# Projection tiles computed one token half after the other, with weight rings of 4, 4 and 2 tiles

## The chip, the cores and the metric

The kernel runs on one core of a Trainium2 chip. The metric is the time of one execution on the device in microseconds. The engines that matter are TensorE (matmuls; PE in the profile, its weight loads PEld), VectorE (DVE), ScalarE (ACT), GpSimd (POOL), and SyncE (SP), which issues all loads and stores. Each engine works through its own stream of instructions in order and waits for the others by semaphores.

## What is computed

A trunk of two layers over 1024 tokens with 1024 channels, and one RMSNorm at the end. Each layer normalises x, applies a shift and scale that depend on the conditioning vector c, makes one wide projection, feeds its columns to three causal mixers (pooling, retention, RWKV-7), gates and merges their results, projects once more and adds the result to x:

```python
h = rms_norm(x, norm_g) * (1.0 + scale) + shift
proj = h @ w_in
pool_u, pool_g, q, k, v, ret_g, rw, rw_g, gate_logits = jnp.split(proj, points, axis=-1)
o_pool = causal_pool_mixer(pool_u, pool_w, pool_scale) * jax.nn.silu(pool_g)
o_ret = retention(q, k, v, positions, ret_norm_g) * jax.nn.silu(ret_g)
o_rwkv = rwkv7_time_mix(rw, shift_mu, w0, w2, a0, a2, k_k, k_a, r_k, ln_w, ln_b) * jax.nn.silu(rw_g)
branches = jnp.stack([o_pool, o_ret, o_rwkv], axis=2)
y = jnp.einsum('btnw,nwd->btnd', branches, w_branch)
merged = jnp.sum(gates * y, axis=2)
return x + gate * (merged @ w_out)
```

The retention mixer applies a rotary embedding to q and k; the RWKV mixer carries a state along the tokens and solves a small triangular system for each chunk of 64 tokens.

## The kernel before

**Layout.** Activations lie with channels on the partitions and tokens along the free dimension, in two halves of 512 tokens (h = 0 and 1). A projection tile is 128 output channels for all 1024 tokens. For numerical accuracy each operand is kept as a high and a low part (`hi`, `lo`), and each product takes three matmuls (`mm1`, line 413): high by high, high weight by low activation, low weight by high activation. With 8 groups of 128 input channels a tile half takes 24 matmuls of 512 columns, a tile 48.

**Weights.** A tile's weights come in two parts of 128 x 512 (j = 0 and 1, four input groups each). `wprep` (line 377) prepares the next tile: for each part a load into a raw tile (tag `wr`, line 406), then `split` (line 426): a cast on ScalarE into the high part (tag `wh`) and a subtraction on POOL into the low part (tag `wl`). Each tag is a ring of three buffers, `bufs=3`. `wprep` is called once as each tile begins, so the weights of one tile are prepared while the tile before is multiplied. Other users of the rings are the loads of the small matrices for RWKV (`lora_load`, line 905), the raw weights of the startup (`wdma`, line 1023), and six tiles of conditioning weights in the startup, which borrow the rings `wh` and `wl` (line 1174). In the second layer's output projection, and for the first three tiles, the split parts go to other buffers (`wout`, `wG`, `wbig`), but the raw tile always comes from `wr`.

**Accumulators.** Results collect in PSUM in a rotation of three tiles (`acc_ps`, line 423). A tile's two halves need one each. An accumulator is free once the tile's evacuation, `evac` (line 984), has read it: for gates a tanh on ScalarE and a store; for the silu gates a tanh and a VectorE operation; for k, r, v a scaled and shifted copy; for retention's q and k (`rotary`, line 885) four VectorE operations per half (lines 891 to 894) and an addition on POOL, with sines and cosines loaded from device memory.

**Background chains.** The mixers are Python generators (`pool_task`, `ret_task`, `rwkv_task`, `rwkv_post`, `norm_task`) in lanes. After each matmul of a projection tile, `pump` (line 292) emits further steps of those whose due time has come, by a clock that counts the matmuls emitted (`mmul`, line 315) and delays that each step gives by hand. So their matmuls stand among those of the projection tiles in TensorE's stream, and their VectorE, ScalarE and POOL work among the evacuations. In the RWKV chain, after the preparation of a head (ending in products of BK and AR, lines 686 to 700, and transposes `bt`), VectorE solves the triangular systems in 30 steps (lines 756 to 766, tiles MT and tm), transposes the result (line 769), and TensorE takes it up (`m`, lines 778 to 797). In startup the order on TensorE, VectorE, ScalarE and POOL is that of the program (line 1124); after it, and for SP throughout, the framework that builds the kernel places each engine's instructions itself, by the order of the program, the buffers that are free and its own estimate of when an instruction can start.

**Stages.** The startup lasts to about 100 us. Then, for each layer, come the projection tiles with the chains in the background (lines 1274 to 1287), the merge stage (1350 to 1388), in which gate and `wg` tiles alternate with branch tiles of 48 matmuls, and the output projection (1399 to 1443), whose tiles take one token half, 24 matmuls. Projection tiles are computed by `in_tile2` (line 1267), which multiplies both halves by the weights' first part, then both by the second, and returns two accumulators; `in_tile` (line 1261) does one half and serves the first three tiles of the second layer.

Of the kernel before, what the change touches and what calls it, by code (L numbers as in the profile page):

```python
# [9 lines left out]
F32 = mybir.dt.float32  # L10
F32R = mybir.dt.float32r
# [6 lines left out]
P = 128  # L18
# [3 lines left out]
W = 512  # L22
HF = 512
# [66 lines left out]
def trunk_kernel(ctx, tc, xT, cvec, pos, vecs, consts, w_ada, w_all, pool_w, lora_w, out):  # L90
# [3 lines left out]
    wp = ctx.enter_context(tc.tile_pool(name="wp", bufs=2))  # L94
# [12 lines left out]
    def nm(s):  # L107
        uid[0] += 1
        return f"{s}_{uid[0]}"
# [26 lines left out]
    def r8(s):  # L136
        return rp.tile([P, 2048], F32, tag="r8", name=nm(s))
# [54 lines left out]
    def ada_load(l, g, slot_, ws, n):  # L192
        for _ in range(n):
            w = slot_("wada")
            nc.sync.dma_start(out=w, in_=w_ada[l, ADA[g][2] + len(ws)])
            ws.append(w)
# [131 lines left out]
    def kept(l):  # L328
        return l + 1 == L
# [47 lines left out]
    def wprep(big=False):  # L377
        for l, it in planner:
            if it != ("merge",):
                break  # L380
            wready.append((it, None))
        else:
            return
        t = None
        if it[0] == "out" and it[1] >= 2 and kept(l):
            if it[2]:
                wready.append((it, keep_w[it[1]]))
                return
            if it[1] < 6:
                t = r8("wout")  # L390
            else:
                if it[1] == 6:
                    keep_w["G"] = gp.tile([P, 32, P], F32, tag="G", name=nm("wG")).rearrange("p a b -> p (a b)")
                t = keep_w["G"][:, 2048 * (it[1] - 6) : 2048 * (it[1] - 5)]
        elif big:
            t = r8("wbig")
        parts = []
        for j in range(2):
            if t is not None:
                o = j * D  # L400
                hi, lo = t[:, o : o + HF].bitcast(F32R), t[:, o + HF : o + D].bitcast(F32R)
            else:
                hi = wp.tile([P, HF], F32R, tag="wh", name=nm("wh"), bufs=3)
                lo = wp.tile([P, HF], F32R, tag="wl", name=nm("wl"), bufs=3)
            raw = wp.tile([P, HF], F32, tag="wr", name=nm("wr"), bufs=3)
            nc.sync.dma_start(out=raw, in_=w_all[l, ITEMS.index(it[:2] if it[0] == "out" else it), j])
            split(raw, hi, lo)
            parts.append((hi, lo))
        if it[0] == "out":
            keep_w[it[1]] = parts  # L410
        wready.append((it, parts))

    def mm1(ps, w, k, r, start, stop):
        (whi, wlo), (rh, rl) = w, r
        for j, (a, b) in enumerate(((whi, rh), (whi, rl), (wlo, rh))):
            mmul(ps, a[:, k * P : (k + 1) * P], b, start=(start and j == 0), stop=(stop and j == 2))
            pump()

    def mm3(ps, w, rhs, start, stop):
        for k in range(4):  # L420
            mm1(ps, w, k, rhs[k], start and k == 0, stop and k == 3)

    def acc_ps():
        return ps_a.tile([P, HF], F32, tag="acc", name=nm("acc"))

    def split(src, hi, lo, eng=nc.gpsimd):
        nc.scalar.copy(hi, src)  # L427
        eng.tensor_tensor(lo, src, hi.bitcast(F32), op=ALU.subtract)  # L428
# [471 lines left out]
    def enter_layer(l):  # L900
        nonlocal L_
        L_ = (l, {}, {}, [])
        L_[3].extend(lora_load(l))

    def lora_load(l):
        raw = wp.tile([P, W], F32, tag="wr", name=nm("lraw"), bufs=3)
        nc.sync.dma_start(out=raw, in_=lora_w[l])
        lw = [cp.tile([P, W], F32R, tag=f"lw{j}", name=nm("lw")) for j in range(2)]
        split(raw, *lw, nc.vector)
        return lw  # L910
# [110 lines left out]
    wraw = {}  # L1021

    def wdma(j, *tiles):
        for i in tiles:
            if j == 0:
                wbig.append(r8("wbig"))
            wraw[j, i] = wp.tile([P, HF], F32, tag="wr", name=nm("wr"), bufs=3)
            nc.sync.dma_start(out=wraw[j, i], in_=w_all[0, i, j])

    def wsp(j, *tiles):  # L1030
# [93 lines left out]
    with tc.manual_schedule(engines={ET.PE, ET.DVE, ET.Activation, ET.Pool}):  # L1124
# [8 lines left out]
        aload(0, 4)  # L1133
        nc.sync.dma_start(out=vec[0], in_=vecs[0])
        wdma(0, 0)
        wsp(0, 0)
        xdma(0, 0, 1)
        wdma(0, 1, 2)
        xdma(1, 0, 1)
        aload(1, 4)  # L1140
# [19 lines left out]
        for h in range(2):  # L1160
            for kt in (2, 3):
                steps(gs[2], 2)
                scaled(h, kt)
                sq(h, kt)
        mms(0, 2, 3)
        wdma(1, 0, 1, 2)
        xdma(0, 4, 5, 6, 7)
        nc.sync.dma_start(out=cst, in_=consts[:, 0 : CST["bone"]])
# [4 lines left out]
        mms(1, 3)  # L1173
        for tag in ("wh", "wl"):
            for _ in range(3):
                w = wp.tile([P, HF], F32, tag=tag, name=nm("wada"), bufs=3)
                ada_load(0, 3, lambda _: w, aw[3], 1)
        aload(3, 2)
        for kt in range(4, 8):
# [3 lines left out]
        for kt in range(4, 8):  # L1183
            sq(1, kt)
            scaled(1, kt)
            steps(gs[3], 2)
        wprep(True)
        aload(4, 8)
        r0 = rstd_task([ssum[0]], rbc[0])
# [24 lines left out]
        next(sb)  # L1214
        first = [wready.popleft()]
        wprep()
        first.append(wready.popleft())
        pss = {}
# [24 lines left out]
    for i in range(3):  # L1243
        first_raw(1, i)
        first_evac(1, i)
    run(sb)
    L_[3].extend(lora_load(0))
    wprep()
    evac(first[0][0], pss[0, 1], 1)
    for h in range(2):  # L1250
# [5 lines left out]
    for l in range(L):  # L1256
        if l:
            enter_layer(l)
        hs = h_cur

        def in_tile(ws, h):
            ps = acc_ps()
            for j in range(2):
                mm3(ps, ws[j], hs[h][4 * j : 4 * j + 4], j == 0, j == 1)
            return ps

        def in_tile2(ws):
            pss = [acc_ps(), acc_ps()]
            for j in range(2):
                for h in range(2):  # L1270
                    mm3(pss[h], ws[j], hs[h][4 * j : 4 * j + 4], j == 0, j == 1)
            return pss

        if l:
            first = [wready.popleft() for _ in range(3)]
# [7 lines left out]
        while wready[0][0] != ("merge",):  # L1283
            it, ws = wready.popleft()
            wprep()
            for h, ps in enumerate(in_tile2(ws)):
                evac(it, ps, h)
# [62 lines left out]
        while wready[0][0][0] != "out":  # L1350
            it, ws = wready.popleft()
            prefetch()
            wprep()
            if it[0] == "wg":
                for h, ps in enumerate(in_tile2(ws)):
                    evac(it, ps, h)
            elif it[0] == "gate":
                n, d = it[1], it[2]
                for h, ps in enumerate(in_tile2(ws)):
                    nc.scalar.activation(gate_tile((n, d, h)), ps, AF.Tanh, scale=0.5)  # L1360
# [38 lines left out]
        for part, (h, sl) in enumerate(parts):  # L1399
# [3 lines left out]
            for i, d in enumerate(out_order(l, part)):  # L1403
                it, ws = wready.popleft()
# [145 lines left out]
```

## Time and profile before

| | us |
|---|---|
| median of three runs | 2542.19 |
| lowest and highest run | 2536.8, 2552.02 |
| the profiled execution | 2541.85 |
| its span, first to last instruction | 2540.1 |
| mean granted TensorE clock, share of full speed | 0.975 |

A row of the stage view gives the stretch in us, its length, for each engine its busy time and instructions, the granted clock, the share of time that the DMA engines were busy, and their rate. A row of waits gives the engine that stood idle and its line, behind the arrow what ended the idle time, then the sum in us, how many times, and the longest. A row in order of time gives start, duration, engine, line, operation, what it writes and reads, and in brackets the idle time before it and what ended that. A group or tile row gives durations in ns as least, median and greatest. Matmuls are pipelined: a matmul of 512 columns is shown as 0.39 us long, but the next begins before it ends, so the pace is read from one start to the next.

### The profile page before, as it was taken

How to read it: one execution, taken by the hardware profiler on the slowest of the kernel's cores; microseconds unless marked ns; L12 is line 12 of the kernel's file. 1: busy time of each engine (PE TensorE's matmuls, PEld its weight loads, DVE VectorE, ACT ScalarE, POOL GpSimd, SP SyncE). 2: the span in 40 equal slices, each digit the busy share in tenths (PEclk: the TensorE clock that was granted, in tenths of full speed). 3: DMA queues.
4: the chain of work that ended last, by engine and by line, in shares of the span. 5: the costliest groups of instructions: out<-in, count | busy, mean ns of one | idle time of the engine just before them, and what ended most of it. 6: DMA issues, size and time to landing. Idle time of an engine off the chain costs nothing. (4 is left out here: it accounts for less than half of the span.)

```text
span 2540.1 us, 35021 instructions
## 1 busy us (share of the span) xinstructions
PE 2421.4 (95%) x13318; PEld 1994.7 (79%) x13318; DVE 1406.1 (55%) x2618; ACT 846.9 (33%) x1530; POOL 846.7 (33%) x729
## 2 busy tenths in 40 slices
PE   6899998989899999999999999999999999999998
PEld 5677876877787788888887778778778778888888
DVE  7986579467646622444464944865783472122244
ACT  4652251333235222222354223322423433222243
POOL 5422323242123124553452313323322222445241
PEclk9899999999899899999999999999999999999999
DMA  6221111111014215663540211211111222553152
GB/s 236 71 69 59 56 42 60 35 54 51 30 51 139 94 63 185 210 193 121 174 134 26 66 35 39 63 39 59 46 42 55 83 84 71 165 159 120 58 154 75
DMA packets 125752, 226.56 MB, mean 89 GB/s; under 512 B 14224, under 2 KB 17552, under 8 KB 125584
## 3 DMA queue, kind: packets, MB, share of 16 engines
q1 hardware_dynamic: 125584, 224.32, 28.1%
q8 instruction: 105, 1.72, 0.3%
q14 instruction: 63, 0.52, 0.1%
HBM read 180.23 MB, written 44.04 MB: 88 GB/s over the span
## 5 line engine op out<-in xcount | busy, mean ns | idle before, releaser
L428 POOL TENSOR_TENSOR wl<-wr,wh 128x512 fp32r<-128x512 f32 x338 | 452.2, 1339 | 1196.0 <-ACT wh L427 1121.2
L319 PE MATMUL acc<-hhi,wh 128*128 128x512 f32 x1968 | 802.2, 408 | 13.2 <-DVE rot L894 11.2
L319 PE MATMUL acc<-hlo,wh 128*128 128x512 f32 x1968 | 802.5, 408 | 0.0
L319 PE MATMUL acc<-hhi,wl 128*128 128x512 f32 x1968 | 800.2, 407 | 0.0
L319 PEld LDWEIGHTS acc<-hhi,wh 128*128 128x128 f32 x1968 | 376.8, 191 | 82.4 <-issue 14.3
L427 ACT CAST wh<-wr 128x512 fp32r<-128x512 f32 x338 | 209.3, 620 | 693.8 <-PE acc L319 509.4
L319 PEld LDWEIGHTS acc<-hhi,wl 128*128 128x128 f32 x1968 | 376.7, 191 | 66.5 <-issue 1.8
L319 PEld LDWEIGHTS acc<-hlo,wh 128*128 128x128 f32 x1968 | 376.6, 191 | 66.5 <-issue 3.1
L319 PE MATMUL acc<-oG,wl 128*128 128x512 f32 x384 | 151.0, 393 | 0.0
L319 PE MATMUL acc<-oG,wh 128*128 128x512 f32 x384 | 151.0, 393 | 0.0
L319 PE MATMUL acc<-olo,wh 128*128 128x512 f32 x384 | 150.9, 393 | 0.0
L825 DVE TENSOR_TENSOR xst<-cy,MT 64x128 f32<-64x128 f32 x128 | 36.1, 282 | 170.2 <-PE cy L319 169.7
L836 DVE SCALAR_TENSOR_TENSOR S<-ch,pc,SP 64x64 f32<-64x64 f32 x256 | 72.4, 283 | 94.8 <-PE ch L319 90.2
L822 ACT ACTIVATE SP<-S,pc 128x128 f32<-128x128 f32 x128 | 51.4, 402 | 210.7 <-DVE S L836 197.4
L759 DVE TENSOR_TENSOR tm<-MT 64x30 f32<-64x30 f32 (+14 forms) x240 | 101.5, 423 | 7.1
L765 DVE TENSOR_TENSOR MT<-MT,tm 64x30 f32<-64x30 f32 (+14 forms) x240 | 96.3, 401 | 7.0
L1377 DVE SCALAR_TENSOR_TENSOR gs<-gs,acc 128x512 f32<-128x512 f32 x64 | 43.7, 684 | 91.7 <-PE acc L319 82.0
L319 PEld LDWEIGHTS ch<-xst,G 128*128 128x128 f32 x512 | 75.5, 191 | 15.9 <-DVE xst L825 6.6
L831 DVE COPY Z<-ch 64x128 f32<-64x128 f32 x128 | 36.0, 282 | 93.0 <-PE ch L319 92.1
L319 PEld LDWEIGHTS cy<-Z,G 128*128 128x128 f32 x512 | 76.4, 190 | 11.1
L319 PEld LDWEIGHTS acc<-oG,wl 128*128 128x128 f32 x384 | 72.1, 188 | 16.5
L319 PEld LDWEIGHTS acc<-oG,wh 128*128 128x128 f32 x384 | 72.1, 188 | 16.5
(298 smaller groups left out, 3888.9 us busy)
## 6 DMA issues: line engine op xcount, KB each, us to landing
wr<-in_w_all SPq DMA_DIRECT2D x364, 256.0 KB, 2.7
wada<-in_w_ada SPq DMA_DIRECT2D x70, 256.0 KB, 3.0
gd<-gsg SPq DMA_DIRECT2D x70, 256.0 KB, 2.0
gs<-gd SPq DMA_DIRECT2D x70, 256.0 KB, 2.8
ol<-od SPq DMA_DIRECT2D x64, 256.0 KB, 3.0
cs<-rope_d SPq DMA_DIRECT2D x32, 256.0 KB, 2.7
ringG<-in_w_ada SPq DMA_DIRECT2D x26, 256.0 KB, 5.4
x<-in_xT SPq DMA_DIRECT2D x16, 256.0 KB, 5.4
```

The source lines that it names most:

```text
L319: nc.tensor.matmul(out, lhsT=lhsT, rhs=rhs, start=start, stop=stop, **kw)
L427: nc.scalar.copy(hi, src)
L428: eng.tensor_tensor(lo, src, hi.bitcast(F32), op=ALU.subtract)
L759: nc.vector.tensor_tensor(pr, M3[:, i + 1 :, i : i + 1].to_broadcast([64, n, i]), M3[:, i : i + 1, 0:i].to_broadcast([64, n, i]), op=ALU.mult,
L765: nc.vector.tensor_tensor(M3[:, i + 1 :, 0:i], M3[:, i + 1 :, 0:i], pr, op=ALU.add)
L822: nc.scalar.activation(SP, S, AF.Copy, scale=pcc)
L825: nc.vector.tensor_tensor(xst[0:64, :], cy[0:64, 0:P], AV[:, c * P : (c + 1) * P], op=ALU.add)
L831: nc.vector.tensor_copy(Z[0:64, c, :], ch[0:64, 0:P])
L836: nc.vector.scalar_tensor_tensor(Sn[rw, rw], ch[rw, P + 64 * hd : P + 64 * hd + 64], pc[rw, c : c + 1], SP[rw, rw], op0=ALU.mult, op1=ALU.add,
L1377: nc.vector.scalar_tensor_tensor(s, s, 1.0, ps, op0=ALU.add, op1=ALU.mult)
```

## The change

`in_tile2` becomes a generator: it computes the first token half with all 24 matmuls, hands its accumulator out, and computes the second half once the caller comes back. Its callers (lines 1286, 1355, 1359) evacuate each half as they get it, so a half's evacuation is now emitted between the halves' matmuls. The accumulator of the second half is taken when its matmuls begin, not at the start of the tile. The rings `wh` and `wl` get four buffers each, the raw ring `wr` two instead of three. A buffer holds 512 values of 4 bytes per partition.

```diff
@@ -400,9 +400,9 @@
                 o = j * D
                 hi, lo = t[:, o : o + HF].bitcast(F32R), t[:, o + HF : o + D].bitcast(F32R)
             else:
-                hi = wp.tile([P, HF], F32R, tag="wh", name=nm("wh"), bufs=3)
-                lo = wp.tile([P, HF], F32R, tag="wl", name=nm("wl"), bufs=3)
-            raw = wp.tile([P, HF], F32, tag="wr", name=nm("wr"), bufs=3)
+                hi = wp.tile([P, HF], F32R, tag="wh", name=nm("wh"), bufs=4)
+                lo = wp.tile([P, HF], F32R, tag="wl", name=nm("wl"), bufs=4)
+            raw = wp.tile([P, HF], F32, tag="wr", name=nm("wr"), bufs=2)
@@ -903,7 +903,7 @@
     def lora_load(l):
-        raw = wp.tile([P, W], F32, tag="wr", name=nm("lraw"), bufs=3)
+        raw = wp.tile([P, W], F32, tag="wr", name=nm("lraw"), bufs=2)
@@ -1024,7 +1024,7 @@
-            wraw[j, i] = wp.tile([P, HF], F32, tag="wr", name=nm("wr"), bufs=3)
+            wraw[j, i] = wp.tile([P, HF], F32, tag="wr", name=nm("wr"), bufs=2)
@@ -1173,7 +1173,7 @@
         for tag in ("wh", "wl"):
             for _ in range(3):
-                w = wp.tile([P, HF], F32, tag=tag, name=nm("wada"), bufs=3)
+                w = wp.tile([P, HF], F32, tag=tag, name=nm("wada"), bufs=4)
@@ -1265,11 +1265,8 @@
         def in_tile2(ws):
-            pss = [acc_ps(), acc_ps()]
-            for j in range(2):
-                for h in range(2):
-                    mm3(pss[h], ws[j], hs[h][4 * j : 4 * j + 4], j == 0, j == 1)
-            return pss
+            for h in range(2):
+                yield in_tile(ws, h)
```

## The prediction

> **What bounds the kernel now.** I read the page first, then the busy time by stage, then who waits for whom on TensorE, then single stalls in order of time.
>
> ```profile
> span 2540.1 us, 35021 instructions
> PE 2421.4 (95%) x13318; PEld 1994.7 (79%) x13318; DVE 1406.1 (55%) x2618; ACT 846.9 (33%) x1530; POOL 846.7 (33%) x729
> core 0: us, PE busy (x) PEld busy (x) DVE busy (x) ACT busy (x) POOL busy (x), PEclk, DMA share, GB/s
> 0.00:100.00 100.00, 67.98 (x249) 53.01 (x250) 85.67 (x114) 44.74 (x74) 58.37 (x48) 0.83 0.53 182
> 100.00:900.00 800.00, 756.21 (x4421) 615.00 (x4420) 520.88 (x1022) 282.01 (x507) 221.50 (x202) 0.96 0.20 61
> 900.00:1345.00 445.00, 445.00 (x2098) 370.49 (x2097) 195.25 (x314) 136.93 (x245) 192.36 (x155) 1.00 0.49 153
> 1345.00:2100.00 755.00, 720.12 (x4337) 589.13 (x4336) 471.27 (x931) 255.56 (x463) 212.48 (x196) 0.99 0.17 54
> 2100.00:2541.00 441.00, 432.09 (x2223) 367.07 (x2221) 133.01 (x238) 127.71 (x242) 161.97 (x128) 0.99 0.38 115
> ```
>
> TensorE bounds it: 2421.4 of 2540.1 us. The edit changes no matmul, so it can win only the idle 118.7 us and the time at a reduced clock. By stage the idle time is 32.0 us in the startup (100 less 67.98), 43.8 and 34.9 us in the two projection stages (100 to 900 and 1345 to 2100), none in the first merge and output stage (445.00 of 445.00), and 8.9 us in the last window. The edit works where nothing is idle, too, but there it has nothing to win, so all that counts is the 78.7 us of the projection stages. Who TensorE waits for there:
>
> ```profile
> PE acc L319 <- DVE rot L894: 11.2, 5, 3.1
> PE bt L323 <- DVE BK L700: 9.9, 9, 2.8
> PE m L319 <- DVE MT L769: 9.6, 3, 4.7
> PE pps L319 <- DVE pdl L428: 9.4, 6, 4.7
> PE nps L319 <- DVE ksl L664: 6.8, 8, 1.8
> PE rot L323 <- DVE yc L570: 5.8, 3, 3.0
> PE acc L319 <- DVE silu L914: 1.8, 2, 1.3
> ```
>
> The first and the last row are the accumulators: a new tile half waits for a PSUM slot that VectorE has not emptied. The five rows between are the mixers' background chains: TensorE reaches a matmul of theirs before VectorE has made its input. No row has wh or wl as what TensorE waits for: the weights have never been late.
>
> **The order of the matmuls.** Three accumulators rotate. Now a tile takes two at once, and its first half ends at matmul 36 of 48; that slot is wanted again at matmul 13 of the next tile, 24 matmuls later. After the edit each half runs through its own 24 matmuls, and a slot is wanted again after the two halves that follow, 48 matmuls later. Two rows give the pace, and the stalls show what the short cycle costs:
>
> ```profile
> 1448.37 0.39 PE L319 MATMUL acc<-hhi,wh 128*128 128x512 f32 x1
> 1448.60 0.39 PE L319 MATMUL acc<-hlo,wh 128*128 128x512 f32 x1
> 1452.06 0.47 PE L319 MATMUL acc<-hhi,wh 128*128 128x512 f32 x1 [3.08 <-DVE rot L894]
> 1453.05 0.63 PE L319 MATMUL acc<-hhi,wh 128*128 128x512 f32 x1
> 1453.47 0.63 PE L319 MATMUL acc<-hlo,wh 128*128 128x512 f32 x1
> ```
>
> Start to start is 0.23 us, so the time that an evacuation has goes from 24 x 0.23 = 5.5 us to 11 us, while the longest wait is 3.1 us. All accumulator waits should vanish: 11.2 + 1.8 = 13.0 us. After the stall of 3.08 us the matmuls start 0.42 us apart instead of 0.23, and the window that holds it shows a granted clock of 0.90 (below). I count some 20 such slow matmuls behind the three longest of these stalls, 20 x 0.19 = 4 us at most.
>
> [...]
>
> **What is late next.** Three of the rot stalls' neighbourhoods, by busy time, with the stalls in them:
>
> ```profile
> 540.00:566.00 26.00, 19.56 (x88) 15.07 (x87) 25.45 (x37) 9.80 (x15) 14.60 (x12) 0.98 0.24 72
> 605.00:665.00 60.00, 49.63 (x264) 40.96 (x263) 55.20 (x104) 7.89 (x14) 16.39 (x13) 0.91 0.17 49
> 1425.00:1476.00 51.00, 41.14 (x214) 33.22 (x213) 48.73 (x89) 7.19 (x12) 16.77 (x13) 0.90 0.22 68
> 547.41 0.47 PE L319 MATMUL acc<-hhi,wh 128*128 128x512 f32 x1 [1.76 <-DVE rot L894]
> 618.50 0.47 PE L319 MATMUL acc<-hhi,wh 128*128 128x512 f32 x1 [2.68 <-DVE rot L894]
> 1435.09 0.47 PE L319 MATMUL acc<-hhi,wh 128*128 128x512 f32 x1 [2.58 <-DVE rot L894]
> 1472.21 0.99 PE L319 MATMUL m<-MT,G 32*32 32x32 f32 x25 [4.21 <-DVE MT L769]
> ```
>
> VectorE is busy for 25.45 + 55.20 + 48.73 = 129.4 of 137 us there, 94%. In the last window TensorE loses 2.58 and 3.08 us to accumulators and then 4.21 us to the end of the triangular solve (MT, lines 753 to 776), which VectorE has worked on all along. If TensorE comes there 5.66 us earlier, it waits some 5.7 us longer, unless VectorE has that much less to do before. So of the four stalls in saturated windows, 1.76 + 2.68 + 2.58 + 3.08 = 10.1 us, I give 94% back, 9.5 us: net of the accumulators 13.0 - 9.5 = 3.5 us. Bounds: 0 (all comes back) to 13.0 (nothing). Of the clock's 4 us I keep 1.5, since a stall that only moves takes its slow matmuls along; bounds 0 and 4.
>
> **The evacuations in halves.** A rotary half costs VectorE four operations, of these shapes:
>
> ```profile
> L893 DVE SCALAR_TENSOR_TENSOR rot<-acc,cs x32: 692/693/694, 273.0 to 1842.0; 64x512 f32<-64x512 f32 x32
> L894 DVE TENSOR_TENSOR rot<-acc,cs x32: 683/683/687, 273.7 to 1842.7; 64x512 f32<-64x512 f32 x32
> ```
>
> 4 x 0.69 = 2.75 us. Today both halves' evacuations are emitted behind the tile's last matmul, up to 5.5 us of VectorE in a row; after the edit it is 2.75 us twice, half a tile apart, with the chains' steps (which are emitted after every matmul) between them. The chains' waits in the list come to 9.9 + 9.6 + 9.4 + 6.8 + 5.8 = 41.5 us in 29 waits, 1.4 us each, less than the 2.75 us by which a burst shrinks; but only 16 tiles are rotary (two kinds, four heads, two layers), and where VectorE is saturated a smaller burst wins nothing. No row shows the new order, so I bound it: at best two thirds of the waits outside the solve, 2/3 x 31.9 = 21 us; at worst the same operations get ahead of the chains and cost 15 us (a rival below). I take a quarter of the 41.5, 10.4 us, nearer the gain because a burst can only get shorter.
>
> **The weight rings.** Per weight half tile: a load, a cast on ScalarE into wh, a subtraction on POOL into wl.
>
> ```profile
> ACT wh L427 <- PE acc L319: 509.4, 183, 10.7
> SPq L406 <- POOL wl L428: 1353.1, 304, 31.9
> L427 ACT CAST wh<-wr x338: 602/621/636, 76.5 to 2514.6; 128x512 fp32r<-128x512 f32 x169
> L428 POOL TENSOR_TENSOR wl<-wr,wh x338: 1255/1292/3169, 77.2 to 2515.3; 128x512 fp32r<-128x512 f32 x169
> wr<-in_w_all SPq DMA_DIRECT2D x364, 256.0 KB, 2.7
> ```
>
> With halves in sequence, the first weight half is in use up to matmul 36 instead of 24. In rings of three its successor could be cast only 12 matmuls, 2.7 us, before it is needed, against 0.62 + 1.29 = 1.9 us of work: too close. In rings of four both casts find slots that the tile before last has left, so a cast has about a tile (11 us). ScalarE then stands less often before a cast that TensorE still blocks (509.4 us in 183 waits now), which frees the silu and square operations queued behind it; I count nothing for it, since no TensorE wait above names ScalarE.
>
> The ring of raw tiles goes from three to two. A slot turns in 2.7 + 0.62 + 1.29 = 4.6 us, with the issue about 5: two slots give a raw tile every 2.5 us. Projection tiles eat one in 5.5 us. The tight place is the output stage of the first layer, 24 matmuls a tile, a raw tile every 2.72 us:
>
> ```profile
> 1228.00:1272.00 44.00, 44.00 (x203) 36.70 (x203) 12.60 (x16) 13.78 (x23) 21.66 (x17) 1.00 0.48 148
> 1234.86 3.04 SPq L406 DMA_DIRECT2D wr<-in_w_all  x2
> ```
>
> It fits by 0.2 us a tile, and the longer wh ring lets each be made 2.7 us earlier. SP runs in order, and a load that waits for its slot holds the state and gate stores behind it; it waits that way today (1353.1 us in 304 waits) without TensorE noticing. I take 0; bounds 0 and +14 us (below).
>
> In the startup the third raw load, issued at 4.97 us with the second, must now wait until POOL has split the first:
>
> ```profile
> 4.97 0.90 SPq L1028 DMA_DIRECT2D wr<-in_w_all  x2
> 8.80 1.26 POOL L428 TENSOR_TENSOR wbig<-wr,wbig 128x512 fp32r<-128x512 f32 x1 [7.59 <-ACT wbig L427]
> 17.82 0.50 PE L319 MATMUL acc<-hlo,wbig 128*128 128x512 f32 x1 [2.03 <-DVE hlo L1042]
> x<-in_xT SPq DMA_DIRECT2D x16, 256.0 KB, 5.4
> ```
>
> It goes out at 10.1 us, lands by 15.5 (5.4 us at that time of the run), and is split by 17.4, while TensorE waits for VectorE until 17.82 anyway. Behind the load on SP stand x and ada loads: if the framework leaves them there, they come up to 4.7 us late. I take +1, bounds 0 and +5.
>
> **The sum**, against the profiled execution (span 2540.1, 2541.85 us in all, 0.3 below the median 2542.19 of the runs): -3.5 - 1.5 - 10.4 + 0 + 1 = -14.4, that is 2527.5; I write **2527**. Own range 2512 to 2538.
>
> **Rivals.**
> 1. *All comes back.* VectorE sets the projection stages' pace, and the stalls only change their names. For it: 94% in the windows above. Against it: VectorE is at 520.88 of 800 us over the whole stage. The clock's 1.5 us against the startup's 1: 2541.
> 2. *The chains lose their place* (slower). First-half evacuations are now emitted ahead of all chain steps that fall into the second half, and VectorE runs in order: a solve step or BK product that fed a matmul in the second half waits up to 2.75 us more at a rotary tile. 16 tiles x 2.75 = 44 us at most; a third of it, 14.7, gives 2556. It decides once the chain has less than 2.75 us in hand, and the waits above say that it often has none. Against it: the second half's burst shrinks by as much.
> 3. *Two raw slots are too few* (slower). If a slot's turn exceeds 2 x 2.72 = 5.44 us, at 6.0 (a late landing, SP held by a store, a POOL subtraction at its 3.17 us) each raw tile comes 0.28 us late: 32 in the first layer's output stage, 16 in the second's, 13.4 us, 2555. Against it: the lead that the wh ring adds.
> 4. *The smaller bursts free most of the waits*: 21 + 13 + 4 us, 2504.
> 5. The framework orders each engine's stream by its own estimate of readiness outside the startup and may undo the halves' order: no change, counted with 1.
>
> **Numbers.** Chances: forecast 0.46, rival 1 with 5 0.14, rival 2 0.18, rival 3 0.12, rival 4 0.08, other slowdowns 0.02. A measurement of this kernel tells 0.5% (12.7 us) from no change. Of the forecast's 0.46 I put 0.38 beyond that bound and 0.08 within. Faster 0.38 + 0.08 = 0.46; same 0.08 + 0.14 = 0.22; slower 0.18 + 0.12 + 0.02 = 0.32. The range takes in rivals 2 and 3 and goes down to rival 4: 2504 to 2562.
>
> **What would show it.** Right: no TensorE wait of acc for rot or silu; the waits of m, bt, pps, nps and rot on VectorE at about 30 us in sum; the windows with idle TensorE still those with VectorE above 90%; ScalarE's wait of wh for acc far below 509 us; the first merge and output stage still without idle time. Wrong: TensorE waits for wh or wl; idle time in the output stage (rival 3); longer chain waits at rotary tiles (rival 2); the same idle sum under other names (rival 1); a first projection matmul that comes later than now.

## The result and the profile after

The changed kernel takes 2560.51 us (median of 7 runs, 2556.86 to 2567.34), the kernel before 2542.19 us (median of 7 runs, 2536.8 to 2552.02). The ratio is 1.0069 with an interval of 1.0046 to 1.0092: slower, by about 18 us, where a gain of 15 was forecast. Of all the executions behind the numbers of this document one, of the kernel after_pps3_m further down, took 4344.88 us at a granted clock of 0.83, and its ratio leaves it out. The page of the changed kernel begins so:

```profile
span 2556.7 us, 35053 instructions
PE 2420.6 (95%) x13318; PEld 1993.8 (78%) x13318; DVE 1408.0 (55%) x2618; ACT 847.8 (33%) x1531; POOL 844.8 (33%) x729
```

TensorE is busy as long as before (2420.6 against 2421.4 us). Its idle time grew from 118.7 to 136.1 us (span less busy), and those 17.4 us are the whole loss of the profiled execution (16.6 us of span). By stage, in the windows of the prediction:

```profile
0.00:100.00 100.00, 70.25 (x253) 54.28 (x254) 83.45 (x111) 43.91 (x73) 60.37 (x49) 0.81 0.52 180
100.00:900.00 800.00, 746.96 (x4451) 608.38 (x4450) 527.73 (x1030) 285.43 (x514) 219.13 (x202) 0.97 0.20 62
900.00:1345.00 445.00, 442.37 (x2066) 368.04 (x2066) 192.29 (x309) 135.68 (x242) 191.02 (x155) 0.99 0.49 152
1345.00:2100.00 755.00, 712.23 (x4142) 582.92 (x4141) 466.32 (x929) 250.37 (x455) 210.90 (x194) 0.97 0.17 53
```

The figure behind the window's length is TensorE's busy time. It is 756.21 - 746.96 = 9.3 us and 720.12 - 712.23 = 7.9 us shorter in the two projection stages and 2.6 us shorter in the window with the first merge and output stage, which ends in the next layer's first tiles; the startup has 2.3 us more. So the idle time grew where the prediction had looked for the gain. In the first layer it didn't yet cost time: at 1345 us both kernels have done as many matmuls (249 + 4421 + 2098 = 6768 before, 253 + 4451 + 2066 = 6770 after), since the kernel before spent the end of its first projection stage at a lower clock. The window from 860 to 900 us, before and after:

```profile
860.00:900.00 40.00, 39.29 (x274) 30.82 (x274) 10.74 (x19) 8.73 (x16) 3.84 (x3) 0.66 0.13 44
```

```profile
860.00:900.00 40.00, 38.82 (x332) 31.56 (x331) 17.57 (x37) 11.26 (x22) 5.12 (x4) 1.00 0.19 60
```

Idle time and clock (the third figure from the end, 0.66 against 1.00) must be read side by side in this kernel. Whom TensorE waits for, shorter rows and those of the startup left out:

```profile
PE pps L319 <- ACT pdh L427: 21.4, 7, 9.1
PE bt L323 <- DVE BK L700: 15.2, 11, 2.5
PE m L319 <- DVE MT L769: 10.2, 3, 5.6
PE pps L319 <- DVE pdl L428: 10.0, 6, 3.7
PE rvt L323 <- DVE rsm L586: 9.0, 5, 3.9
PE nps L319 <- DVE ksl L664: 4.6, 7, 0.9
PE bt L323 <- ACT wh L427: 3.0, 1, 3.0
PE rot L323 <- DVE yc L570: 1.9, 3, 1.2
PE acc L319 <- DVE rot L894: 1.7, 1, 1.7
```

Two rows of the kernel before that the prediction didn't show; the second makes 13.7 us of waits for pps with the pdl row there:

```profile
PE rvt L323 <- DVE rsm L586: 4.7, 3, 2.7
PE pps L319 <- ACT pdh L427: 4.3, 3, 2.1
```

The accumulators' waits fell as forecast, from 13.0 us (rot 11.2, silu 1.8) to 1.7. The chains' waits did the opposite of the forecast: bt, m, pps, nps, rot and rvt together were 9.9 + 9.6 + 13.7 + 6.8 + 5.8 + 4.7 = 50.5 us and are 15.2 + 10.2 + 31.4 + 4.6 + 1.9 + 9.0 = 72.3 us. That is 21.8 us more against 11.3 less; what is left of the 17.4 us lies in shorter rows. The row of bt with wh isn't a wait for weights: this matmul, at 170.62 us, reads BK, which is complete at 170.47, and a cast into wh ends at nearly the same time.

The longest new wait, 9.11 us, shows how the two hang together. In both kernels the second layer's stage begins at the same time (its first bt matmuls, which wait for BK, start at 1376.72 us before and 1376.52 after), and both then run to the same matmul of the pool chain, pps. First the windows of the kernel before up to that matmul, then those of the changed one, with its wait as a window of its own:

```profile
1376.00:1428.70 52.70, 51.27 (x274) 40.12 (x274) 36.09 (x59) 21.39 (x35) 16.23 (x17) 1.00 0.15 47
1428.70:1456.80 28.10, 22.44 (x84) 17.64 (x83) 26.95 (x47) 2.56 (x5) 11.67 (x9) 0.88 0.24 70
```

```profile
1376.00:1427.80 51.80, 50.76 (x273) 40.04 (x273) 33.51 (x55) 20.81 (x35) 14.31 (x15) 1.00 0.14 42
1427.80:1446.57 18.77, 16.76 (x73) 13.30 (x72) 18.14 (x29) 2.10 (x4) 9.16 (x7) 1.00 0.23 71
1446.57:1455.68 9.11, 0.00 (x1) 0.00 (x1) 8.75 (x16) 0.62 (x1) 2.81 (x2) 0.66 0.29 87
```

And the instructions at the end of these stretches, of the kernel before and of the changed one (start, duration, engine, operation, and in brackets the idle time before it):

```profile
1449.05 0.68 DVE L532 SCALAR_TENSOR_TENSOR pd<-pt,pu 128x512 f32<-128x512 f32 x1
1455.18 0.63 PE L319 MATMUL pps<-pdh,pw 128*128 128x512 f32 x1
```

```profile
1446.73 0.68 DVE L894 TENSOR_TENSOR rot<-acc,cs 64x512 f32<-64x512 f32 x1
1454.24 0.68 DVE L532 SCALAR_TENSOR_TENSOR pd<-pt,pu 128x512 f32<-128x512 f32 x1
1455.01 0.62 ACT L427 CAST pdh<-pd 128x512 fp32r<-128x512 f32 x1 [12.50 <-DVE pd L532]
1455.68 0.80 PE L319 MATMUL pps<-pdh,pw 128*128 128x512 f32 x1 [9.11 <-ACT pdh L427]
```

Before, TensorE lost 2.58 and 3.08 us to accumulators on the way, ran slow matmuls behind both (0.43 us apart; clock 0.88 in that window) and came to pps at 1455.18, when pd had long been made (1449.05). Now it has neither, but a wait of 2.00 us for pdl and five matmuls fewer on the way (344 instead of 349, some 1.1 us); it comes at 1446.57, 8.6 us earlier, and stands there until 1455.68. VectorE is busy throughout (18.14 of 18.77 and 8.75 of 9.11 us) and makes pd 5.2 us later than before. All 8.6 us are given back, and 0.5 us more. The stretch that follows is slower, too, here before and after,

```profile
1456.80:1500.00 43.20, 38.99 (x329) 32.09 (x328) 23.08 (x45) 11.16 (x21) 6.02 (x6) 0.92 0.11 35
```

```profile
1455.68:1500.00 44.32, 40.89 (x299) 33.08 (x300) 23.53 (x43) 9.76 (x17) 7.31 (x6) 0.76 0.12 36
```

and it holds 30 matmuls fewer in 1.1 us more, at a clock of 0.76 instead of 0.92. In finer windows, in the changed kernel:

```profile
1455.68:1460.00 4.32, 4.32 (x11) 3.44 (x12) 4.17 (x7) 0.59 (x1) 2.10 (x1) 0.53 0.21 61
1460.00:1472.00 12.00, 11.27 (x50) 8.96 (x48) 10.75 (x27) 2.33 (x4) 2.57 (x2) 1.00 0.21 66
1472.00:1492.00 20.00, 17.31 (x169) 13.98 (x170) 6.89 (x8) 3.50 (x6) 1.26 (x1) 0.57 0.05 15
```

Right behind the long wait only some 4 us run at 0.53. The rest of the low clock (0.57 from 1472 to 1492 us) lies in the stretch of the triangular solve, whose matmuls start at 1474.69 us behind a wait of 3.43 us for MT; before, it came behind 4.21 us, and from 1472 to 1500 us the clock was 0.88. From there on the rest of the 16.6 us comes in small steps, at waits such as 2.13 us for pps (up to 1605.90 us), 2.51 for rkt (up to 1684.88) and 3.85 for rvt (up to 1888.53), until the second projection stage ends.

### The profile page after: what moved, and what is told of

Same layout as the page of the kernel before. It is cut to its first block, busy times and chain, and to the rows that moved or that the text cites. A ratio compares the mean times of both kernels' runs of the same rounds, so it can differ in the third digit from the quotient of the medians.

```text
span 2556.7 us, 35053 instructions
## 1 busy us (share of the span) xinstructions
PE 2420.6 (95%) x13318; PEld 1993.8 (78%) x13318; DVE 1408.0 (55%) x2618; ACT 847.8 (33%) x1531; POOL 844.8 (33%) x729
## 4 chain that ended last, share of the span: by engine, by line
PE 68%; DVE 22%; issue 3%; ACT 3%; DMA 2%; POOL 1%; SPq 0%; DVEq 0%; ACTq 0%; POOLq 0%
PE acc L319 53%; PE ch L319 3%; PE cy L319 3%; DVE MT L765 3%; DVE tm L759 3%; DVE ksq L677 2%; PE m L319 1%; PE av L319 1%; PE g L319 1%; DVE Lc L668 1%; DMA wr<-in_w_all 1%; DVE ada_acc L212 1%; PE ro L319 1%; DVE MT L749 1%; DVE BK L686 0%
## 5 line engine op out<-in xcount | busy, mean ns | idle before, releaser
L836 DVE SCALAR_TENSOR_TENSOR S<-ch,pc,SP 64x64 f32<-64x64 f32 x256 | 72.3, 282 | 96.8 <-PE ch L319 93.2
L765 DVE TENSOR_TENSOR MT<-MT,tm 64x30 f32<-64x30 f32 (+14 forms) x240 | 102.3, 426 | 7.0
L319 PE MATMUL acc<-hhi,wbig 128*128 128x512 f32 x224 | 82.2, 444 | 3.5 <-ACT hhi L1083 2.3
```

The source lines that it names most:

```text
L319: nc.tensor.matmul(out, lhsT=lhsT, rhs=rhs, start=start, stop=stop, **kw)
L765: nc.vector.tensor_tensor(M3[:, i + 1 :, 0:i], M3[:, i + 1 :, 0:i], pr, op=ALU.add)
L836: nc.vector.scalar_tensor_tensor(Sn[rw, rw], ch[rw, P + 64 * hd : P + 64 * hd + 64], pc[rw, c : c + 1], SP[rw, rw], op0=ALU.mult, op1=ALU.add,
```

## Experiments

All ran against the kernel before on the same chip; every ratio is given with its interval. The kernels named "halves" and "pairs" have the matmul order of the changed kernel and of the kernel before; the digits are the rings of wh, wl and raw tiles. The order in which the tiles are taken is the same in all, except where a line says that a gate tile moves.

### The parts alone: halves_333, pairs_442, late_442

halves_333 is the changed kernel with the rings put back:

```
-                hi = wp.tile([P, HF], F32R, tag="wh", name=nm("wh"), bufs=4)
+                hi = wp.tile([P, HF], F32R, tag="wh", name=nm("wh"), bufs=3)
...
```

> The changed kernel with the rings back at 3, 3, 3: only the order by halves. Theory A (evacuations emitted between the halves put the mixers' chains later on VectorE and ScalarE): stays slow, 2555 to 2565, with the wait of pps for pdh at some 20 us as in the changed kernel (21.4; before 4.3). Theory B (two raw tiles hold SP's queue and the weights): back to 2527 to 2542, that wait below 8 us. With wh in rings of three, a cast has only 12 matmuls, 2.7 us, for 1.9 us of work, so TensorE may wait for wh or wl here: up to +10 us on top of either.

Measured: 2557.32 us, ratio 1.0076 (1.0054 to 1.0098). Its waits are those of the changed kernel (pps 21.3 and 10.3, bt 15.2, rvt 9.0 us). The order alone makes the loss. With rings of three, which the prediction thought too close for the new order, TensorE waits for wl for 0.9 us in all.

pairs_442 is the kernel before with the new rings.

> The kernel of before with the rings at 4, 4, 2: only the rings. Theory A: 2540 to 2545, waits as before (acc for rot 11.2 us, pps for pdh 4.3). Theory B: 2553 to 2562, with waits of ScalarE's cast for the raw load in the projection stages and a longer wait of pps for pdh.

Measured: 2545.57 us, ratio 1.0022 (1.0011 to 1.0034): a small loss. TensorE waits 15.5 us for BK in 12 waits instead of 9.9 in 9, and is busy for 441.70 instead of 445.00 us between 900 and 1345 us. The rings alone cost about a third of the loss, and beside the new order nothing that shows (the changed kernel's ratio is 1.0069, that of halves_333 1.0076). Theory B falls.

late_442 is the changed kernel with both evacuations written behind all 48 matmuls:

```
         def in_tile2(ws):
-            for h in range(2):
-                yield in_tile(ws, h)
+            return [in_tile(ws, h) for h in range(2)]
```

> The changed kernel, but both halves' accumulators are handed out together after 48 matmuls, so both evacuations are emitted after the tile, as before: the order of the matmuls and the rings without the new place of the evacuations. Theory A: 2535 to 2545, accumulator waits below 5 us, pps for pdh below 8 us. Theory B: stays at 2555 to 2565.

Measured: 2561.57 us, ratio 1.0081 (1.0058 to 1.0104). Theory A, that the place where the first evacuation is written costs the time, falls in this form: it stands where it stood before, and nothing is regained. The instruction streams say why. The framework arranges each engine's stream by its own estimate of when operands are ready, so an accumulator that is complete 12 matmuls earlier pulls its evacuation forward wherever it was written. Counted over VectorE's chain operations, 307 have more evacuation operations ahead of them in the changed kernel than before, and 15 fewer; in late_442 still 238 against 16; in pairs_442 4 against 13. The count says that the stream has changed, not what that costs.

### Which tiles: rot_halves, rest_halves

rot_halves gives the new order to the 16 rotary tiles alone, rest_halves to all others (rings 3, 3, 3):

```
-        def in_tile2(ws):
+        def in_tile2(ws, it):
+            if it[0] in ("rq", "rk"):
+                for h in range(2):
+                    yield in_tile(ws, h)
+                return
...
```

> The kernel before, rings 3, 3, 3; only the 16 rotary tiles (rq, rk) run their matmuls by token halves, all other tiles in pairs as before. Theory C (the rotary evacuations, 2.75 us of VectorE per half, become ready 12 matmuls earlier and take VectorE ahead of the chains' steps): the 11.2 us of acc waits on rot vanish, the pps waits on pdh and pdl grow from 13.7 us to some 25, and the time is most of the way to the changed kernel, 2550 to 2556. Theory D (any tile's new order moves the evacuations against the chains' hand-written delays; rotary tiles are nothing special): a part by their number, 16 of about 85 tiles, 2544 to 2547. The prediction's own view (shorter bursts free the chains) would have it at 2535 or below.

> The complement: rings 3, 3, 3; rq and rk tiles in pairs, all other two-half tiles by token halves. Theory C: little of the loss, 2542 to 2547, the acc waits on rot stay at 11 us. Theory D: most of the loss, 2551 to 2556, with the pps waits at 20 us or more.

Measured: 2554.24 us, 1.0051 (1.0032 to 1.0070), and 2555.10 us, 1.0063 (1.0043 to 1.0082). Each part alone costs most of what the whole does (1.0076): 0.51 and 0.63% of 0.76. Theory C, that the rotary evacuations with their 2.75 us are the cause, explains the first and not the second; theory D has the second right and the first too small. The parts don't add up, and no kind of tile is the culprit. The two also bear on another rival, ScalarE's stream, into which the evacuations put their tanh and copies: in rot_halves no chain operation of ScalarE has changed its place against the evacuations, and the time is lost; in pairs_442 nearly all have (590 of 608), and the loss is 0.2%.

### The place in the tile: fin24, fin30, fin36, fin45

Four kernels that differ in one number, a. The evacuations are written where they stood before, the rings are 3, 3, 3; the last three matmuls of the first half are put so that its accumulator is complete after matmul 24, 30, 36 or 45 of the tile (a = 0, 2, 4, 7):

```
-            for j in range(2):
-                for h in range(2):
-                    mm3(pss[h], ws[j], hs[h][4 * j : 4 * j + 4], j == 0, j == 1)
+            seq = [(0, k) for k in range(7)] + [(1, k) for k in range(a)] + [(0, 7)]
+            for h, k in seq + [(1, k) for k in range(a, 8)]:
+                mm1(pss[h], ws[k // 4], k % 4, hs[h][k], k == 0, k == 7)
```

> One series of four kernels: rings 3, 3, 3, both evacuations written behind the tile's 48 matmuls as in the kernel before, only the place of the first half's last three matmuls varies, so that its accumulator is complete after matmul 24, 30, 36 or 45 of 48 (36 in the kernel before, 24 in the changed one). Here: 24. Theory R (the framework orders VectorE's stream by its own estimate of when an operand is ready; an accumulator that is complete earlier puts its evacuation ahead of chain steps, 233 of VectorE's chain operations get more evacuations ahead of them, 14 fewer): as slow as the changed kernel, 2551 to 2562, few acc waits, longer chain waits. Theory S (what costs is the spans of the weight tiles: the first weight half stays in use until matmul 33 to 42 instead of 24, and the rings turn later): the same here.

> Complete after matmul 30. In VectorE's stream 147 chain operations have more evacuations ahead of them than in the kernel before, 7 fewer. Theory R: between, 2545 to 2555. Theory S: 2551 to 2562.

> Complete after matmul 36, as in the kernel before, though 21 matmuls of the first half run in one go. VectorE's stream is that of the kernel before but for 3 places. Theory R: no change, 2538 to 2545, with acc waits on rot back at 9 to 13 us and pps waits on pdh and pdl at 12 to 17. Theory S: 2551 or more.

> Complete after matmul 45. 223 chain operations have fewer evacuations ahead of them, 5 more. Theory R: the chains' waits (pps, bt, m, rvt, nps) fall below the kernel before's 44 us, the acc waits grow over its 13; net 2530 to 2546. Theory S: 2551 or more. Theory D (the kernel before is an optimum of its delays, and any new deal costs): 2548 or more.

| complete after matmul | chain operations with more / fewer evacuations ahead | median us | ratio |
|---|---|---|---|
| 24 | 233 / 14 | 2564.70 | 1.0095 (1.0067 to 1.0122) |
| 30 | 147 / 7 | 2562.88 | 1.0081 (1.0058 to 1.0104) |
| 36 | 1 / 2 | 2543.42 | 1.0018 (1.0000 to 1.0037) |
| 45 | 5 / 223 | 2562.02 | 1.0064 (1.0042 to 1.0087) |

fin36 does almost the whole first half in one go, keeps the first weight half in use longer than the kernel before, and costs 0.18%, with an interval that begins at zero; moving three matmuls by 6 or 12 places costs 20 us. So it is neither the halves nor the weights, but when the first accumulator is complete, and with it VectorE's stream: theory S falls. Theory R has 36 right and 24 in kind (2.7 us above its range). It misses 30, which it put between the two at 2545 to 2555 us, and 45, where the chains are ahead of more evacuations than before and the time is lost all the same. Theory D has that one right, as far as the median goes: four of fin45's 12 runs take 2542 to 2552 us.

How the time is lost isn't the same everywhere. The second lines of the pages of fin24 and fin36, with the first lines above them:

```profile
span 2560.6 us, 35005 instructions
PE 2429.8 (95%) x13318; PEld 2001.7 (78%) x13318; DVE 1405.3 (55%) x2618; ACT 846.7 (33%) x1530; POOL 844.2 (33%) x729
```

```profile
span 2543.2 us, 35026 instructions
PE 2413.1 (95%) x13318; PEld 1988.8 (78%) x13318; DVE 1408.2 (55%) x2618; ACT 845.7 (33%) x1530; POOL 848.0 (33%) x729
```

TensorE is idle for 130.8 us in the one and 130.1 in the other; of the 17.4 us between their spans 16.7 lie in its busy time (2429.8 against 2413.1), and as the matmuls are the same 13318, that is the clock: 0.970 against 0.977 over the run. The other runs agree: the median granted clock is 0.970 to 0.971 for fin24, 0.973 to 0.974 for fin30, 0.977 to 0.978 for fin36 and 0.971 for fin45, whose four shortest runs have 0.974 to 0.979 and the other eight 0.965 to 0.971. The changed kernel against the kernel before loses by idle time; fin24 against fin36 by slower matmuls. fin36's own chain waits in this profile (pps 12.5 + 3.5, bt 16.2, m 12.7 us) aren't those of the kernel before either, though VectorE's stream is: the median is the same, the waits are dealt anew.

### The delays: halves_pps4000, pairs_pps4000

Each chain step is written so many nanoseconds of the program's own clock behind the one before, by numbers in the code. Here the delay between the split of pd and the pps matmuls is raised, in the new and in the old order:

```
             split(d, dh, dl, nc.vector)
-            yield 1500
+            yield 4000
             ps = mx("pps")
```

> All tiles by token halves, rings 3, 3, 3, and the pool chain's delay between the split of pd and the pps matmuls raised from 1500 to 4000 ns of the program's own clock, so that TensorE comes to pps 2.5 us later; the order in which the tiles are taken stays the same. If the pps waits (31.6 us, 14 of the growth over the kernel before) are what costs: they fall below 10 us and the time goes from 2557 to 2535 to 2545. If the lost time only moves to the next wait in VectorE's queue: pps falls, others grow by about as much, 2552 or more.

> The control: the kernel before with the same delay of 4000 ns. Its pps waits are 13.7 us. If the waits are worth their length: 2530 to 2534, and the gap to the run above shrinks to under 8 us. If they only move: 2540 to 2545.

Measured: 2548.70 us, 1.0045 (1.0024 to 1.0067), and 2549.65 us, 1.0030 (1.0012 to 1.0048). None of the four expectations holds: the new order gains about half of the loss, and the old one gets slower. The page of halves_pps4000 and its waits for m and pps:

```profile
span 2554.1 us, 35036 instructions
PE 2431.2 (95%) x13318; PEld 2006.3 (79%) x13318; DVE 1399.3 (55%) x2618; ACT 847.4 (33%) x1530; POOL 845.7 (33%) x729
```

```profile
PE m L319 <- DVE MT L769: 18.3, 4, 9.0
PE pps L319 <- DVE pdl L428: 10.3, 5, 4.5
PE pps L319 <- ACT pdh L427: 4.3, 4, 1.4
```

The pps waits fell from 31.6 to 14.6 us, 8.4 us of that went to the solve (m from 9.9 to 18.3), and the idle time from 134.0 (halves_333) to 122.9 us. But busy time rose from 2421.0 to 2431.2 us at a clock of 0.967: in this execution the saving came back as slower matmuls. It is 7 us slower than the kernel's median; over all runs the median clock is 0.971 against 0.975 to 0.976 for halves_333. In the control, too, idle time hardly moved (121.7 us) and busy time grew by 5.9.

### Two delays together: pairs_m, halves_pps3_m, after_pps3_m, pairs_pps3_m, halves_pps3_m_bt

The second delay stands ahead of the solve's matmuls (m):

```
-        yield 4500
+        yield 7000
         for q in range(2):
             ps = mx("m1")
```

> The control: the kernel before with the delay ahead of m at 7000 ns alone (one gate tile moves). Its m waits are 9.6 us. If waits are worth their length: 2532 to 2538; if they are handed on, or if any new deal of the delays costs: 2542 or more.

> All tiles by token halves, rings 3, 3, 3, the delay before the pps matmuls raised from 1500 to 3000 ns and the one before the solve's matmuls (m) from 4500 to 7000 ns; one gate tile moves to another place in the order of the tiles. If the loss is the waits and the clock that long ones leave: pps and m waits together fall from 41.5 us (31.6 and 9.9 with rings of three) to under 20, no others grow by more than 5, and the time is 2535 to 2546. If VectorE's order hands the stall on: rvt, rot, ro or acc waits take it over and the time is 2548 to 2560.

> The changed kernel as it is, rings 4, 4, 2, with the two delays of halves_pps3_m (3000 ns before pps, 7000 before m). The rings cost 0.2 per cent on the old order: if they add up, 2543 to 2550, with a TensorE wait on wh or in the layer transition; if the delays regain the whole loss of the changed kernel, 2537 to 2543.

> The control: the kernel before with the same two delays. If the delays are worth as much on the old order as on the new one (17 us): 2525 or less. If each order has its own best delays and the old one's are near theirs: 2540 to 2552, slower than halves_pps3_m.

> halves_pps3_m with the delay before the bt transposes raised from 1500 to 2500 ns as well (its bt waits are 15.7 us); three gate tiles move. If waits are worth their length: bt under 9 us, 2530 to 2537, faster than both kernels. If handed on: 2540 or more.

| kernel | order, rings | pps, m delay | median us | ratio |
|---|---|---|---|---|
| pairs_m | pairs, 3 3 3 | 1500, 7000 | 2546.90 | 1.0020 (1.0004 to 1.0035) |
| halves_pps3_m | halves, 3 3 3 | 3000, 7000 | 2540.52 | 0.9987 (0.9973 to 1.0001) |
| after_pps3_m | halves, 4 4 2 | 3000, 7000 | 2540.18 | 0.9991 (0.9977 to 1.0005) |
| pairs_pps3_m | pairs, 3 3 3 | 3000, 7000 | 2540.45 | 0.9996 (0.9981 to 1.0011) |
| halves_pps3_m_bt | halves, 3 3 3; bt delay 2500 | 3000, 7000 | 2541.56 | 0.9998 (0.9984 to 1.0011) |

In all five one gate tile or more stands at another place in the order (three in the last); what that does by itself no run shows. With 4000 and 7000 ns the new order has no time: that program, halves_pps_m, deadlocks. halves_pps3_m has the whole loss back, by two numbers that touch no matmul and no evacuation of the tiles, but for that gate tile. Its page and its waits, from its fastest run (2534.79 us):

```profile
span 2533.0 us, 35050 instructions
PE 2410.3 (95%) x13318; PEld 1988.2 (78%) x13318; DVE 1403.4 (55%) x2618; ACT 847.5 (33%) x1530; POOL 843.7 (33%) x729
```

```profile
PE bt L323 <- DVE BK L700: 15.7, 9, 4.4
PE rvt L323 <- DVE rsm L586: 11.0, 3, 7.6
PE pps L319 <- ACT pdh L427: 10.2, 3, 5.9
...
PE pps L319 <- DVE pdl L428: 8.2, 3, 4.2
```

pps and m waited 41.5 us in halves_333; here pps has 18.4 and m has no row. rot grew by 5.0 and rvt by 2.0 us, and rkt and yt have waits of 3.4 and 2.9 us that weren't there. Idle time is 122.7 us and the clock 0.977. By the count of above 667 chain operations of VectorE have more evacuations ahead of them here than in the kernel before, 6 fewer, and in the control pairs_pps3_m 429 against 21: more than in the changed kernel, at no loss. after_pps3_m shows that the rings' share disappears with it, though they cost 0.2% on the old order. And the control says what was regained: with the same delays the old order takes 2540.45 us, no more and no less. The expectation that it would stay behind halves_pps3_m, because each order has its own best delays, isn't borne out, and neither is the hope of a gain of 17 us there.

pairs_m lost its m waits (9.6 to 2.5 us), but rvt took 7.1 us more and the clock was lower (0.973 in the median of its runs against 0.976 for those of the kernel before beside it); the expectation of 2542 us or more holds there. That waits are handed on holds for halves_pps3_m_bt: bt fell to 8.5 and rvt to 2.9 us, m came back with 9.1, and the time is what it was.

So four kernels of both orders and both rings end between 2540.2 and 2541.6 us, within 0.13% of the kernel before. No version beats it by what can be measured.

## Why the prediction was wrong

Point by point, in the prediction's own steps:

- **The accumulators (13.0 us).** Right. Their waits went to 1.7 us, for the reason given: a slot has 48 matmuls instead of 24.
- **What is late next (94% of 10.1 us given back).** Right in kind and nearly in size. In the stretch that held two of the four stalls, the 8.6 us that TensorE came earlier were given back whole, with 0.5 us on top. The place was wrong: the stall went to pps and not to the solve, whose wait stayed (10.2 us against 9.6).
- **The clock (1.5 us).** Over the run it came out at nothing: 0.973 after, 0.975 before, busy time the same to 0.8 us. The stalls that only moved took slow matmuls along, as the prediction had feared, with 0.53 in the 4.3 us behind the 9.11 us.
- **The evacuations in halves (-10.4 us).** This is the step that failed, in sign. The chains' waits grew by 21.8 us; take off the 9.5 us that the step before gives them, and 12.3 us are left where -10.4 was put. The reason given for the gain, "a burst can only get shorter", looked at the length of the evacuation and not at its place. An accumulator complete at matmul 24 has its evacuation put into VectorE's stream ahead of chain steps that used to stand before it, and this hit 307 chain operations against 15 that gained. The prediction's own rival 2 said this with 14.7 us. It had the mechanism as the place where the evacuations are written, and late_442 shows that it is the place where the accumulator is complete. Rival 2's remark that it decides once a chain has less than 2.75 us in hand is too narrow as well: tiles without rotary evacuations cost as much alone (rest_halves).
- **What neither the forecast nor a rival had.** The loss isn't owed to the order as such: with 3000 and 7000 ns (and a gate tile at another place) the same order costs nothing, while the old order gains nothing by them. That the old delays fit the old place of the evacuations is the reading that this leaves, and it fits that moving the accumulator's completion to either side, 30 or 45 instead of 36, costs 0.8 and 0.6%. The prediction took the schedule around the change as something that the change could only relieve.
- **The weight rings (0).** Nearly right: 0.2% alone (5 us, within the bounds 0 and +14), nothing beside the new order. The window with rival 3's output stage lost 2.6 us, but to one wait of 2.63 us at 1320 us, for POOL's part of the norm (rn, line 457); such a wait stands in all four kernels with rings 4, 4, 2.
- **ScalarE's wait of wh for acc, "far below 509 us".** Wrong, and no other step hung on it. The row of the changed kernel:

```profile
ACT wh L427 <- PE acc L319: 533.9, 205, 11.3
```

  With the rings back at three it is 518.9 us, with the longer rings on the old order 553.1: the cast waits wherever it is put, and TensorE doesn't notice. SP's wait for raw tiles became shorter (1184.9 instead of 1353.1 us), that of the gate stores longer (221.6 instead of 150.1).
- **The startup (+1 us).** Nothing was lost there: TensorE is busy for 70.25 of the first 100 us instead of 67.98.

What stays open: why the old delays fit the old order so well (nothing in the code says how they were found), which of the reordered steps cost the time, and what the clock would have done with the solve's matmuls in other places; where it falls is told in the last section.

## What to carry to other kernels

Where background chains are placed by hand-given delays into a stream of matmuls, every edit that moves the time at which an accumulator is complete can reorder the vector engine's queue against these chains: look which operations move ahead of which, not only how long a burst is. How many move doesn't give the price (223 fewer cost 0.6% in fin45, 667 more cost nothing in halves_pps3_m), so try the delays again before the edit itself is judged. A stall that goes away ahead of a saturated engine can come back at another thing that this engine makes, here 8.6 of 8.6 us. And undo the parts of a change in ways that leave its result standing, as fin36 does: half the matmul order was free, and three matmuls' place was the cost.

## What the runs showed of the hardware that was not expected

In the kernel before the granted clock fell to 0.50 in a stretch in which TensorE was not idle. These are windows of 4 us around one of its eight triangular solves; those between 876 and 892 us, left out, have a clock of 0.50 as well:

```profile
864.00:868.00 4.00, 3.29 (x42) 2.61 (x41) 3.97 (x3) 0.43 (x1) 0.00 (x0) 1.00 0.17 61
868.00:872.00 4.00, 4.00 (x39) 3.19 (x38) 1.95 (x2) 1.34 (x3) 1.26 (x1) 0.61 0.14 30
872.00:876.00 4.00, 4.00 (x37) 2.68 (x36) 0.00 (x0) 0.57 (x1) 0.00 (x0) 0.50 0.11 40
...
892.00:896.00 4.00, 4.00 (x11) 3.23 (x12) 0.28 (x1) 1.69 (x3) 1.27 (x1) 0.50 0.18 66
896.00:900.00 4.00, 4.00 (x24) 3.48 (x23) 0.85 (x3) 0.66 (x2) 0.00 (x0) 0.98 0.23 70
```

The third figure from the end is the granted clock. TensorE waits 0.71 us for MT ahead of the first m matmul (866.4 us), then runs the solve's small matmuls (m, 32x32, and av) in batches between the tiles' own, and from 868 us on, for some 28 us in which it is busy for 4.00 of every 4.00 us, its clock is 0.61 in the first window and 0.50 in the next six. In the changed kernel the same solve comes at 872.2 us behind a wait of 1.18 us, the longer of the two, and the clock is 1.00 from there to 912 us.

How often the clock is low at a solve was counted over the eight solves of the 18 profiles of this study, as the mean granted clock of the 40 us from the first m matmul on. Behind 44 solves for which TensorE had waited (0.2 us or more) it is 0.84 in the mean, and 41 of them are below 0.95; behind the 100 for which it had not waited it is 0.977, and 11 are below 0.95. The waits aren't spread evenly: 42 of the 44 lie at the third to fifth solve of a run, and there the 12 solves without a wait have 0.93, against 0.84. So the count doesn't separate the wait from the place, and that a wait lowers the clock isn't shown. The missing share of the clock times 40 us, summed over a profile's solves, comes to 24.5 us in the kernel before, 12.3 in the changed one, 22.8 in fin24 against 12.6 in fin36, 39.2 in halves_pps4000 with its wait of 9.0 us, and 5.7 in halves_pps3_m, where no solve is waited for. Between halves_pps4000 and halves_pps3_m the idle time is the same, 122.9 and 122.7 us; of the 21.1 us between their spans 20.9 are busy time (2431.2 against 2410.3), that is clock, and the medians of their runs agree (0.971 against 0.976 to 0.977). A saving read off the waits alone isn't yet a saving: pairs_m has less idle time than the kernel before (2545.6 - 2431.8 = 113.8 us against 118.7) and is slower, with 10.4 us more of busy time.

In these stretches the clock doesn't go by the length of the idle time alone. Behind the wait of 9.11 us in the changed kernel it is 0.53 for 4.3 us. In the kernel before, behind the stalls of 2.58, 2.68 and 3.08 us, matmuls start 0.42 to 0.43 us apart for some time, and the clock is 0.56 from 1435.09 to 1439.00 us, 0.63 from 618.50 to 623.00 and 0.64 from 1452.06 to 1456.80; at the solve of 866 us, with no wait over 0.71, it is 0.50 from 872 to 896 us. What lowers the clock at the solve no run shows.

From run to run the clock moves as well, and the time with it: fin36's 12 runs span 2538.9 to 2556.6 us at granted clocks of 0.982 to 0.971.
